# Running the 256-column half of an accumulating matmul unit first where the unit before ended on the same width

## The chip, the cores and the metric

The kernel runs on one core of one Trainium2 chip. Five engines work beside each other: TensorE (PE, matrix products; its weight loads are shown apart as PEld), VectorE (DVE), ScalarE (ACT), GpSimd (POOL) and SyncE (SP, which here only issues DMAs). The metric is the device time of one execution in microseconds, the median of several runs.

## The reference

One layer of a streaming encoder over 512 tokens of width 2048, all in fp32. Cut to what matters:

```python
hn   = rmsnorm(x, norm_g)                          # 512 x 2048
proj = einsum('bsd,dc->bsc', hn, w_in)             # 12 x 512 columns q,k,v,gate of 3 branches,
                                                   # 4 forget logits, 3 x 2048 merge-gate columns
ya = forgetting_attention(qa, ka, va, f_logit)     # branch A: softmax with forget bias
yb = chunked_relpos_attention(qb, kb, vb, rel)     # branch B: softmax over a band, relative bias
yc = stick_breaking_attention(qc, kc, vc)          # branch C
ys = stack([ya, yb, yc]) * silu(gate)
up = einsum('bsnw,nwd->bsnd', ys, w_up)            # 3 products 512 -> 2048
merged = sum(sigmoid(merge_gates) * up)
return x + einsum('bsd,de->bse', merged, w_out)    # 2048 -> 2048
```

Nearly all the work is in three dense products: the input projection (2048 by some 12,300 columns), the up-projection and the output projection.

## The kernel before

**Precision by parts.** An fp32 operand is split in two fp32r parts, a high part (`wh` of the weights, rounded by ACT, line 243) and the rest, the low part (`wl`, by DVE as the difference, line 247). A product is high x high + high x low + low x high. For one 128 x 128 block of weights that is a matmul with 512 moving columns for the high weights (256 columns of the operand's high part and 256 of its low part, which lie side by side) and one with 256 columns for the low weights (the operand's high part alone). The first kind is called wide here, the second narrow. All of them are issued in `mm`, line 261, so the profile shows them on line 262, the wide ones with `wh` and the narrow ones with `wl` among their tiles.

**Tiling.** Input and output projections work on pairs of 128-column blocks with a Strassen-like scheme over 2 x 2 blocks of 1024 by 256: seven products instead of eight. `PairTask` is one such pair of column blocks; its seven `Pair` units, one per product, are numbered 1 to 7. A unit has eight steps `j` along the contraction: eight wide matmuls into a PSUM bank, then, once the low weights are there (`yield u.ready`), eight narrow ones into the left half of the same bank. Since the halves of the operand are summed up later, the bank holds two 256-column halves that are folded together when it is read.

**Order and banks.** The usual order of a pair's units is 1, 2, 6, 5, 7, 3, 4. Unit 6 adds onto the bank that unit 1 has left open, 7 onto 6, 4 onto 7, and 3 onto 5 (the table `onto` in `mms_of`); between two such units the bank is read as it stands, by ACT or DVE (`after_of`), and the later unit waits for that reading (`yield self.ev[onto]`). The units 1, 2 and 5 open a bank and clear it with their first matmul (`start`). One of the gate pairs has the order 1, 5, 6, 2, 7, 3, 4 (`x1_first`). Two pairs, the first gate pair and the first output pair, are `late`: their seven units use the banks in turn, don't add on, and issue 24 matmuls of 256 columns each, sixteen with the high weights and eight with the low ones. `single` units do that as well: all units of the late pairs, and unit 4 of the last output pair (`plain_end`).

**Stages.** First the q, k, v and gate columns of one head, taken straight without the scheme; then for the other eleven heads a pair for q and k, a pair of gate columns, a pair for v and the branch gate, and a pair of gate columns, 28 units a head (24 pairs of gate columns in all); then the up-projection, 32 units of 512-column matmuls alone; then eight output pairs. The attention of a head is spread over the units that follow it.

**What sets the order.** The instruction lists of PE, ACT and DVE are written in the order that a planner finds (`Flow`). It has a clock for each of the three engines, costs for the instructions (`mm_us`, `act_us`, `dve_us`) and due times, and always takes the operation that can start first. `stream` (line 1519) goes through the units one after the other and lets attention work slip in between any two matmuls; at unit `i` it starts `prep` of unit `i + 2`, the split of its weights. `wh` and `wl` have three buffers each, which the planner does not count. Raw weights come in by DMA into six tiles, issued on SP's queue; the weights of product 5 and of product 7, sums of two blocks, are added up in the transfer, on POOL's queue. On the chip only the semaphores count; an engine that is early runs ahead of the plan as far as its list allows.

Of the kernel before, what the change touches and what calls it, by code (L numbers as in the profile page):

```python
# [16 lines left out]
S = 512  # L17
# [8 lines left out]
UK = 8  # L26
NQ = 4
HS = S // 2
# [7 lines left out]
PE, ACT, DVE = 0, 1, 2  # L36
# [26 lines left out]
class Flow:  # L63
# [19 lines left out]
    def spawn(self, gen, slack, ready=None):  # L83
        task = Task(gen, slack, self.now if ready is None else ready)
        self.tasks.append(task)
        self.advance(task)
# [62 lines left out]
def mm_us(n, x=1):  # L149
    return x * max(0.115, n / 2400 + 0.0133)  # L150
# [11 lines left out]
def hybrid_kernel(  # L162
# [16 lines left out]
    wp = ctx.enter_context(tc.tile_pool(name="wp", bufs=3))  # L179
    tp = ctx.enter_context(tc.tile_pool(name="tp", bufs=NT))  # L180
    sp = ctx.enter_context(tc.tile_pool(name="sp", bufs=8))
# [10 lines left out]
    flow = Flow()  # L192
    spawn, set_, give = flow.spawn, flow.set, flow.give
    t2s, atts, raws, xps = Slots(NT, KEPT), Slots(4), Slots(NR), Slots(NX)
    accs = [Slots(2), Slots(1), Slots(1)]
# [7 lines left out]
    def acc(i=0):  # L203

        return pa.tile([P, S], F32, tag=f"acc{i}", name=nm("acc"), bufs=1 if i else 2)
# [10 lines left out]
    LH, RH = slice(0, HS), slice(HS, S)  # L216

    def two(ap):

        return ap.rearrange("p (h s) -> p h s", h=2)  # L220

    class Parts:


        def __init__(self, s, ev=None):
            self.t = xp.tile([P, 2, 2, HS], F32R, tag="x", name=nm(s))
            self.hi, self.lo = self.t[:, :, 0, :], self.t[:, :, 1, :]
            self.ev = ev or [Event(), Event()]
# [32 lines left out]
    def mm(ps, w, x, start=False, stop=False, more=False):  # L261
        nc.tensor.matmul(ps, w, x, start=start, stop=stop, skip_group_check=more)  # L262
# [10 lines left out]
    first = []  # L273
# [77 lines left out]
    class Unit:  # L351


        def __init__(self, mms, after=None, shape=(UK, P), srcs=()):
            self.shape, self.mms, self.after, self.srcs = list(shape), mms, after, srcs
            self.ready_hi, self.ready, self.there, self.raw = Event(), Event(), Event(), None

        def source_there(self):
            return self.there
# [24 lines left out]
    def prep(u):  # L384
        n = u.shape[0] * P
        u.hi = wp.tile([P] + u.shape, F32R, tag="wh", name=nm("wh"), bufs=LA + 1)
        u.lo = wp.tile([P] + u.shape, F32R, tag="wl", name=nm("wl"), bufs=LA + 1)
        yield u.source_there()
        yield from split(u.hi, u.lo, u.source(), n, u.ready, hi_ev=u.ready_hi)
        u.split_done()  # L390
# [168 lines left out]
    class Pair(Unit):  # L559


        def __init__(self, task, i):
            super().__init__(task.mms_of(i), task.after_of(i))
            self.task, self.p = task, task.order[i]

        def source_there(self):
            if self is self.task.units[0]:
# [10 lines left out]
    class PairTask:  # L578
# [57 lines left out]
        def mms_of(self, i):  # L636
            p = self.order[i]
            bank = (0, 1, 2, 0, 0, 1, 2)[i] if self.late else {2: 1, 5: 2, 3: 2}.get(p, 0)
            onto = None if self.late else {6: 1, 7: 6, 4: 7, 3: 5}.get(p)
            more = onto is not None  # L640
            single = self.late or self.plain_end and p == 4
            self.bank = getattr(self, "bank", {})
            self.bank[p] = bank

            def go(u):
                if more:
                    yield self.ev[onto]
                    self.ps[p] = self.ps[onto]
                else:
                    yield accs[bank], 1  # L650
                    self.ps[p] = acc(bank)

                for j in range(UK):
                    yield lambda: self.ops[p](j) is not None
                    r, _, ev = self.ops[p](j)
                    yield ev
                    if single:
                        yield PE, mm_us(HS)
                        mm(self.ps[p][:, LH], u.hi[:, j, :], r[:, 0, :], j == 0 and not more, more=more)
                    else:  # L660
                        yield PE, mm_us(S)
                        mm(two(self.ps[p]), u.hi[:, j, :], r, j == 0 and not more, more=more)
                    if single:
                        yield PE, mm_us(HS)
                        mm(self.ps[p][:, LH], u.hi[:, j, :], r[:, 1, :], more=more)
                yield u.ready
                for j in range(UK):
                    yield PE, mm_us(HS)
                    mm(self.ps[p][:, LH], u.lo[:, j, :], self.ops[p](j)[1], stop=j == UK - 1, more=more)
            return go  # L670

        def after_of(self, i):
# [844 lines left out]
            yield from load_unit(u)  # L1517

    def stream():
        for i, u in enumerate(units):  # L1520
            cur[0] = i
            for g in side.pop(i, ()):
                spawn(g(), 5.0, flow.fin)
            for j in range(LA + 1) if i == 0 else (i + LA,):
                if j < len(units):
                    spawn(prep(units[j]), 2.5, flow.fin)
            yield u.ready_hi
            yield from u.mms(u)
            if u.after is not None:
                spawn(u.after(), 0.0, flow.fin)  # L1530
# [6 lines left out]
    for k in range(UK):  # L1537
        spawn(combos(k), 5.0)
    spawn(stream(), 1e9)
    flow.run()  # L1540
    assert not side, side


NT = 21
KEPT = 1
NX = 28
NR = 6
# [47 lines left out]
```

## Time and profile before

| | |
|---|---|
| median of three runs | 1331.93 us (1330.86 to 1333.83) |
| the profiled execution | 1331.46 us, its span 1329.7 us |
| PE busy | 1317.4 us, 99% of the span |
| PE weight loads busy | 1149.0 us, 86% |
| DVE busy | 1134.5 us, 85% |
| ACT busy | 806.3 us, 61% |
| PE in the chain of waits that ended last | 98% |
| DMA | 266.24 MB, mean 200 GB/s |
| wide matmuls on `wh` into pair banks, mean of one | 0.39 us |
| narrow matmuls on `wl`, mean of one | 0.28 us |

The busy share of PE is an overlap of pipelined instructions: a narrow matmul is shown with 0.28 us although the next one starts 0.12 us later. For the pace one reads the starts in the timeline, not the durations. In the timeline, rows with the same tiles and shape are merged: the first number is the start of the first, the second the time from there to the end of the last, and xN their count.

The profiled execution took 1331.46 us, of which 1329.7 are its span from the first to the last instruction and 1.8 lie around it; it is 0.5 us below the median.

### The profile page before, as it was taken

The numbers are of one execution on the slowest core, as the hardware profiler recorded it, in microseconds if no ns is written. First come the engines' busy times: TensorE is split into PE (matmuls) and PEld (weight loads), VectorE is DVE, ScalarE is ACT, GpSimd is POOL, SyncE is SP. The second block draws the span as 40 slices with busy tenths as digits, with TensorE's granted clock in tenths as the row PEclk, the third lists the DMA queues.
The fourth block names the chain that finished last, engine by engine and source line by source line (L and its number), as shares of the span: only waits on it lengthen the run. The fifth ranks groups of instructions, "written<-read, shape, count | busy, mean of one in ns | idle before, by whom it ended". The sixth has DMA issues, their size and how long they took to land.

```text
span 1329.7 us, 20204 instructions
## 1 busy us (share of the span) xinstructions
PE 1317.4 (99%) x7490; PEld 1149.0 (86%) x7490; DVE 1134.5 (85%) x1675; ACT 806.3 (61%) x1280; POOL 94.8 (7%) x120
## 2 busy tenths in 40 slices
PE   8999999999999999999999999999999999999998
PEld 5888888888888888888888888888888888888887
DVE  7899888788888889888988979888899877897786
ACT  8777557575566665666556665666557655454443
POOL 0000000010000100000010100001000000000100
PEclk9999999999999999999999999999999999999999
DMA  9876677767776777767777677676768856668883
GB/s 312 230 188 171 187 201 188 199 171 200 195 209 165 205 204 184 212 158 210 202 182 205 163 207 200 188 202 175 198 179 273 276 193 193 186 173 241 238 238 108
DMA packets 93251, 266.24 MB, mean 200 GB/s; under 512 B 10576, under 2 KB 17360, under 8 KB 93152
## 3 DMA queue, kind: packets, MB, share of 16 engines
q1 hardware_dynamic: 73472, 203.79, 45.6%
q0 software_dynamic: 15552, 56.63, 24.9%
q10 hardware_dynamic: 4128, 4.53, 1.0%
q8 instruction: 59, 0.97, 0.3%
q14 instruction: 40, 0.33, 0.1%
HBM read 245.21 MB, written 19.70 MB: 199 GB/s over the span
## 4 chain that ended last, share of the span: by engine, by line
PE 98%; DVE 1%; DMA 0%; issue 0%; ACT 0%; DVEq 0%
PE acc L262 84%; PE att L262 8%; PE att L998 1%; PE att L257 1%; PE att L258 1%; PE att L1111 1%; PE att L1112 1%; PE att L259 1%; PE att L1110 1%; DVE wl L247 0%; PE att L1062 0%; DMA raw<-in_w_col 0%; PE att L1213 0%; PE att L899 0%; PE att L900 0%; DVE m L247 0%
## 5 line engine op out<-in xcount | busy, mean ns | idle before, releaser
L247 DVE TENSOR_TENSOR wl<-raw,wh 128x1024 fp32r<-128x1024 f32 (+2 forms) x419 | 500.7, 1198 | 145.0 <-ACT wh L243 137.7
L243 ACT ACTIVATE wh<-raw 128x1024 fp32r<-128x1024 f32 (+2 forms) x419 | 434.7, 1038 | 149.3 <-PE acc L262 61.9
L262 PE MATMUL acc<-x,wh 128*128 128x512 f32 (+1 forms) x1568 | 399.4, 391 | 6.8 <-ACT wh L243 6.8
L262 PEld LDWEIGHTS acc<-x,wh 128*128 128x128 f32 x1568 | 277.6, 190 | 55.8 <-ACT wh L243 7.2
L262 PE MATMUL acc<-t,wh 128*128 128x512 f32 (+1 forms) x1128 | 283.8, 390 | 0.0
L262 PEld LDWEIGHTS acc<-t,wh 128*128 128x128 f32 x1128 | 198.3, 189 | 32.8
L262 PEld LDWEIGHTS acc<-x,wl 128*128 128x128 f32 x1504 | 207.0, 190 | 18.0 <-DVE wl L247 1.7
L262 PE MATMUL acc<-x,wl 128*128 128x256 f32 (+1 forms) x1504 | 217.0, 285 | 0.6 <-DVE wl L247 0.6
L262 PEld LDWEIGHTS acc<-t,wl 128*128 128x128 f32 x1104 | 151.7, 190 | 11.4
L262 PE MATMUL acc<-t,wl 128*128 128x256 f32 x1104 | 155.5, 283 | 0.0
L282 POOL DMA_DIRECT2D raw<-in_w_col x92 | 79.5, 864 | 926.7 <-DMA raw<-in_w_col 529.7
L262 PE MATMUL acc<-m,wh 128*128 128x512 f32 (+1 forms) x512 | 113.7, 366 | 1.5 <-DVE m L247 1.5
L262 PEld LDWEIGHTS acc<-m,wh 128*128 128x128 f32 x512 | 85.5, 190 | 14.4 <-DVE m L247 1.9
L805 ACT ACTIVATE c<-acc 128x256 f32<-128x256 f32 x51 | 19.5, 383 | 97.2 <-PE acc L262 94.2
L772 ACT ACTIVATE u<-acc 128x512 f32<-128x512 f32 x51 | 30.3, 594 | 79.4 <-PE acc L262 79.4
L751 ACT ACTIVATE u<-acc 128x512 f32<-128x512 f32 x52 | 31.1, 598 | 72.2 <-PE acc L262 69.3
L627 DVE TENSOR_TENSOR raw<-raw,raw 128x1024 f32<-128x1024 f32 x54 | 65.9, 1220 | 0.5
L621 DVE TENSOR_TENSOR raw<-raw,raw 128x1024 f32<-128x1024 f32 x54 | 65.9, 1220 | 0.4
L262 PE MATMUL att<-y,wh 128*128 128x512 f32 x256 | 65.8, 389 | 0.0
L262 PEld LDWEIGHTS acc<-m,wl 128*128 128x128 f32 x448 | 60.6, 191 | 3.8
L262 PE MATMUL acc<-m,wl 128*128 128x256 f32 x448 | 62.5, 282 | 0.0
L262 PEld LDWEIGHTS att<-y,wh 128*128 128x128 f32 x256 | 48.1, 188 | 10.0
(191 smaller groups left out, 1389.8 us busy)
## 6 DMA issues: line engine op xcount, KB each, us to landing
raw<-in_w_col SPq DMA_DIRECT2D x237, 512.0 KB, 4.3
raw<-in_w_col POOLq DMA_DIRECT2D x92, 512.0 KB, 6.5
raw<-in_w_out SPq DMA_DIRECT2D x40, 512.0 KB, 4.0
gl<-c SPq DMA_DIRECT2D x48, 256.0 KB, 3.6
raw<-in_w_up SPq DMA_DIRECT2D x32, 384.0 KB, 3.8
sg<-gl SPq DMA_DIRECT2D x48, 256.0 KB, 5.1
raw<-in_w_out POOLq DMA_DIRECT2D x16, 512.0 KB, 6.1
x<-in_xT SPq DMA_DIRECT2D x16, 256.0 KB, 6.4
```

Source lines behind the costliest of these rows:

```text
L243: nc.scalar.activation(hi, src, AF.Copy)
L247: nc.vector.tensor_sub(lo, src, f(hi))
L257: nc.tensor.matmul(ps, lh, rh, start=start, stop=False, skip_group_check=more)
L258: nc.tensor.matmul(ps, lh, rl, start=False, stop=False, skip_group_check=more)
L259: nc.tensor.matmul(ps, ll, rh, start=False, stop=stop, skip_group_check=more)
L262: nc.tensor.matmul(ps, w, x, start=start, stop=stop, skip_group_check=more)
L282: nc.gpsimd.dma_start(to, src, accum_op=ALU.add)
L621: nc.vector.tensor_add(w[1], w[1], w[5])
L627: nc.vector.tensor_add(w[2], w[2], w[1])
L751: nc.scalar.activation(self.u, ps, AF.Copy)
L772: nc.scalar.activation(self.s, ps, AF.Copy)
L805: nc.scalar.activation(c, ps[:, RH], AF.Copy, scale=-1.0)
```

## The change

A unit gets a flag `low_first`. Where it is set, the unit issues its eight narrow matmuls first and its eight wide ones behind them; otherwise wide first, as before. `mms_of` is rewritten around two inner functions, `high` and `low`, which get told whether they come first, for the `start` and `stop` marks. `stream` sets the flag for a unit just before it is issued: the unit adds onto an open bank, the unit before ended with narrow matmuls, and the low weights have been ready for 0.4 us by the planner's clock. `single` and `onto` move from the closure to the unit. Nothing else is touched: the same matmuls, operands, banks and loads.

```diff
             self.ready_hi, self.ready, self.there, self.raw = Event(), Event(), Event(), None
+            self.low_first = False
...
             self.task, self.p = task, task.order[i]
+            self.single = task.late or task.plain_end and self.p == 4
+            self.onto = None if task.late else {6: 1, 7: 6, 4: 7, 3: 5}.get(self.p)
...
-                for j in range(UK):
-                    yield lambda: self.ops[p](j) is not None
-                    r, _, ev = self.ops[p](j)
-                    yield ev
-                    if single:
...
-                yield u.ready
-                for j in range(UK):
-                    yield PE, mm_us(HS)
-                    mm(self.ps[p][:, LH], u.lo[:, j, :], self.ops[p](j)[1], stop=j == UK - 1, more=more)
+                def high(first):
+                    for j in range(UK):
+                        yield lambda: self.ops[p](j) is not None
+                        r, _, ev = self.ops[p](j)
+                        yield ev
+                        start, stop = first and j == 0 and not more, not first and j == UK - 1
...
+                            yield PE, mm_us(S)
+                            mm(two(self.ps[p]), u.hi[:, j, :], r, start, stop, more)
+
+                def low(first):
+                    yield u.ready
+                    for j in range(UK):
+                        yield lambda: self.ops[p](j) is not None
+                        _, x, ev = self.ops[p](j)
+                        yield ev
                         yield PE, mm_us(HS)
+                        mm(self.ps[p][:, LH], u.lo[:, j, :], x, first and j == 0 and not more,
+                           not first and j == UK - 1, more)
+
+                steps = (low, high) if u.low_first else (high, low)
+                for first, step in zip((True, False), steps):
+                    yield from step(first)
             return go
...
     def stream():
+        ends_low = False
...
             yield u.ready_hi
+            if isinstance(u, Pair) and not u.single:
+                low_there = u.ready.t is not None and u.ready.t + AHEAD <= flow.clock[PE]
+                u.low_first = ends_low and u.onto is not None and low_there
+                ends_low = not u.low_first
+            else:
+                ends_low = False
             yield from u.mms(u)
...
+AHEAD = 0.4
```

More of the change, by code (lines that the diff above doesn't have):

```diff
@@ L638, in mms_of @@
             bank = (0, 1, 2, 0, 0, 1, 2)[i] if self.late else {2: 1, 5: 2, 3: 2}.get(p, 0)
-            onto = None if self.late else {6: 1, 7: 6, 4: 7, 3: 5}.get(p)
-            more = onto is not None
-            single = self.late or self.plain_end and p == 4
             self.bank = getattr(self, "bank", {})
@@ L645, in go @@
             def go(u):
+                single, onto = u.single, u.onto
+                more = onto is not None
                 if more:
@@ L651, in go @@
                     self.ps[p] = acc(bank)
-                for j in range(UK):
-                    yield lambda: self.ops[p](j) is not None
-                    r, _, ev = self.ops[p](j)
-                    yield ev
-                    if single:
-                        yield PE, mm_us(HS)
[L659 to L663, printed above, removed]
-                        yield PE, mm_us(HS)
-                        mm(self.ps[p][:, LH], u.hi[:, j, :], r[:, 1, :], more=more)
@@ L666, in go @@
-                yield u.ready
-                for j in range(UK):
-                    yield PE, mm_us(HS)
-                    mm(self.ps[p][:, LH], u.lo[:, j, :], self.ops[p](j)[1], stop=j == UK - 1, more=more)
+                def high(first):
[4 more added lines that the diff above has]
+                        start, stop = first and j == 0 and not more, not first and j == UK - 1
+                        if single:
+                            yield PE, mm_us(HS)
+                            mm(self.ps[p][:, LH], u.hi[:, j, :], r[:, 0, :], start, stop, more)
+                            yield PE, mm_us(HS)
+                            mm(self.ps[p][:, LH], u.hi[:, j, :], r[:, 1, :], more=more)
+                        else:
+                            yield PE, mm_us(S)
+                            mm(two(self.ps[p]), u.hi[:, j, :], r, start, stop, more)
@@ L1527, in stream @@
             yield u.ready_hi
+            if isinstance(u, Pair) and not u.single:
+                low_there = u.ready.t is not None and u.ready.t + AHEAD <= flow.clock[PE]
+                u.low_first = ends_low and u.onto is not None and low_there
+                ends_low = not u.low_first
+            else:
+                ends_low = False
             yield from u.mms(u)
```

## The prediction

> **What bounds the kernel now.** I read the page first (busy shares, granted clock, chain of waits), then the busy time by stretches, then TensorE's (PE's) waits, and then the timeline of PE alone, where the price of the change stands.
>
> ```profile
> span 1329.7 us, 20204 instructions
> PE 1317.4 (99%) x7490; PEld 1149.0 (86%) x7490; DVE 1134.5 (85%) x1675; ACT 806.3 (61%) x1280; POOL 94.8 (7%) x120
> PEclk9999999999999999999999999999999999999999
> ```
>
> ```profile
> 64.00:1036.00 972.00, 971.20 (x5684) 855.36 (x5683) 845.51 (x1231) 613.34 (x974) 76.78 (x89) 1.00 0.72 195
> ...
> 1180.00:1329.70 149.70, 144.82 (x851) 128.04 (x849) 115.80 (x151) 63.67 (x76) 11.21 (x13) 1.00 0.72 205
> ```
>
> ```profile
> PE acc L262 <- ACT wh L243: 6.8, 2, 6.6
> PE acc L262 <- DVE m L247: 1.5, 2, 1.3
> PE acc L262 <- DVE wl L247: 0.6, 1, 0.6
> ```
>
> In the 972 us that hold all but one of the column pairs PE is busy for 971.20, at a granted clock of 1.00. In the whole span it waits 8.9 us for other engines, and the longest of those waits lie at the start and at the first output pair. So the time is the length of PE's instruction stream, and whatever shortens this stream reaches the end undiminished, as long as VectorE (DVE, 85% busy) keeps delivering the weights. The stalls at the start and the tail behind the last matmul are not touched by the change.
>
> A busy PE says nothing about pace, so the timeline of starts comes next. This is the plain stretch of ten units, nothing put between them:
>
> ```profile
> 623.66 2.00 PE L262 MATMUL acc<-t,wh 128*128 128x512 f32 x8
> 625.50 1.12 PE L262 MATMUL acc<-t,wl 128*128 128x256 f32 x8
> 626.45 2.00 PE L262 MATMUL acc<-x,wh 128*128 128x512 f32 x8
> ...
> 651.59 0.22 PE L257 MATMUL att<-qkh,qkh 128*128 128x128 f32 x1
> ```
>
> The first column is the start. Eight 512-column matmuls take 625.50 - 623.66 = 1.84 us, eight 256-column ones 626.45 - 625.50 = 0.95 us, and ten units take 651.59 - 623.66 = 27.93 us: **2.793 us a unit**. Now the same widths where they do not alternate. The gated up-projection issues 512 columns only, the first output pair 256 columns only. The first row below is from the chain of waits, the others from the timeline.
>
> ```profile
> 1038.99 5.44 PE att L262 x24
> ```
>
> ```profile
> 1169.54 2.08 PE L262 MATMUL acc<-m,wh 128*128 128x256 f32 x16
> 1171.46 1.12 PE L262 MATMUL acc<-m,wl 128*128 128x256 f32 x8
> ...
> 1181.06 2.08 PE L262 MATMUL acc<-m,wh 128*128 128x256 f32 x16
> ```
>
> 24 wide matmuls in 5.44 us are 226.7 ns each. From 1169.54 to 1181.06 lie four units of 24 narrow ones, 11.52 us or 120.0 ns each. At these paces a unit would take 8 x 226.7 + 8 x 120.0 = 2773.6 ns. It takes 2793, so **one turn from narrow to wide and back costs 19.4 ns**, wholly in the wide part (1.84 against 1.814 us, so some 26 ns lost there; the narrow part is some 10 ns quicker than its steady pace). Both steady stretches cross unit boundaries, weight buffers and banks too, so it isn't the boundary that costs, but the alternation.
>
> The Trainium skill, "TensorE: Matmul & The Clock Gate", section "Back-to-back issue gap", gives an isolated matmul a gap of N/2.4 + 2.5 ns, by its own width alone; an estimate from that is 8 x 215.8 + 8 x 109.2 = 2600 ns for a unit in any order, and the change would save nothing. The trace does not agree in either respect: 2793 ns, and a unit whose cost depends on its neighbours. The same section also says that in a stream of weight loads and matmuls both set the spacing, which fits better.
>
> **The change, part by part.** (1) *Turns removed.* A normal pair runs its units in the order 1, 2, 6, 5, 7, 3, 4. Units 6, 7, 4 and 3 add onto an open bank. The rule makes a unit start with its narrow run only if the unit before ended narrow, so the string of a pair goes from HL HL HL HL HL HL HL (H wide, L narrow) to HL HL LH HL LH HL LH: seven turns become four, at 6, 7 and 4 three fall away. There are 22 column pairs, 24 gate pairs and 8 output pairs; the first gate pair and the first output pair are `late` and excluded, and in the last output pair unit 4 is `single`. That is 52 x 3 - 1 = 155 turns. The gate pair in the order 1, 5, 6, 2, 7, 3, 4 also loses three.
>
> (2) *The condition.* A unit is turned round only if the planner's clock has its low weights ready 0.4 us ahead. The planner's clock is not in the trace, but what really happened is. I set the k-th low-weight split on DVE against the k-th unit on PE over all 156 units 6, 7 and 4. In 114 of them the low weights are there over 2 us before the unit begins, in 18 they are less than 0.53 us early, and none is late. The first of the 18 (a DVE row and a PE row), the last, and the shortest of all:
>
> ```profile
> 382.17 1.22 DVE L247 TENSOR_TENSOR wl<-raw,wh 128x1024 fp32r<-128x1024 f32 x1
> ...
> 383.86 1.32 PE L262 MATMUL acc<-t,wh 128*128 128x512 f32 x5
> ```
>
> ```profile
> 1031.76 1.22 DVE L247 TENSOR_TENSOR wl<-raw,wh 128x1024 fp32r<-128x1024 f32 x1
> ...
> 1033.29 2.00 PE L262 MATMUL acc<-t,wh 128*128 128x512 f32 x8
> ```
>
> ```profile
> 731.92 1.22 DVE L247 TENSOR_TENSOR wl<-raw,wh 128x1024 fp32r<-128x1024 f32 x1
> ...
> 733.38 2.00 PE L262 MATMUL acc<-t,wh 128*128 128x512 f32 x8
> ```
>
> The first split ends at 383.39 and its unit begins at 383.86, 0.47 us later. The second is 0.31 us early, the third 0.24. If the condition refuses all of the 18 and nothing else, 155 - 18 = 137 turns go; if none, 155. I take 141, nearer to the lower end since the planner's figure for a 1024-column split, 1.175 us, leaves DVE no more slack than the trace does. 141 x 19.4 ns = **2.7 us**; the ends are 2.66 and 3.0 us.
>
> (3) *Weights needed earlier.* In a turned unit the low weights are needed 1.84 us earlier than now, and the one wait of 0.6 us for them in the rows above shows how much room there was. A price of nothing rests on the leads in (2). If the lead were short by x, PE would stand for x in that unit; I take 0 for the 137, and 0 to 0.2 us each for up to 18 tight ones (0.4 us is the margin asked, 0.24 the shortest lead seen), so 0 to 3.6 us at the far end, 0.1 us in the sum.
>
> (4) *Buffers freed at other times.* High and low weights rotate through three buffers each. A turned unit gives its low buffer back 1.84 us sooner and its high buffer 0.95 us later, since the wide run ends the unit. The third unit after it then gets its ACT split (`wh`, 1.05 us) up to 0.95 us later, and behind that its DVE split, the return of the raw tile, and the load (on SP's queue, or POOL's for the summed ones) that waits for this tile. What hides it: ACT's split now begins over two units before its use where nothing queues, and where the lead is tight the split has been waiting for DVE rather than for ACT:
>
> ```profile
> 463.06 0.38 ACT L805 ACTIVATE c<-acc 128x256 f32<-128x256 f32 x1 [2.49 <-PE acc L262]
> 463.34 1.05 ACT L243 ACTIVATE wh<-raw 128x1024 fp32r<-128x1024 f32 x1
> ```
>
> ```profile
> 466.76 1.22 DVE L247 TENSOR_TENSOR wl<-raw,wh 128x1024 fp32r<-128x1024 f32 x1
> ```
>
> ```profile
> 468.45 2.00 PE L262 MATMUL acc<-t,wh 128*128 128x512 f32 x8
> ```
>
> This is a unit 6 with 0.47 us of lead. Its high split stood behind an ACT copy that waited for the end of the unit 4 three places before (462.86), so the high buffer of that unit, freed 0.95 us later, would not have moved it, and it was done 2.4 us before DVE came to it. Loads: ACT's splits wait only 5.4 us in the whole span for arriving weights, so I price a later load at 0 as well.
>
> ```profile
> DMA raw<-in_w_col: 5.4, 4
> ```
>
> (5) *Attention work put between.* Where the planner slips score or transpose matmuls into a unit, they would fall after about five narrow matmuls of a turned unit instead of after three wide ones. Both cases are in the trace with the same work (three 128-column products and a mask):
>
> ```profile
> 282.05 0.86 PE L262 MATMUL acc<-x,wh 128*128 128x512 f32 x3
> ...
> 283.07 1.38 PE L262 MATMUL acc<-x,wh 128*128 128x512 f32 x5
> 284.30 1.12 PE L262 MATMUL acc<-x,wl 128*128 128x256 f32 x8
> ```
>
> ```profile
> 113.72 0.64 PE L262 MATMUL acc<-x,wl 128*128 128x256 f32 x4
> ...
> 114.52 0.72 PE L262 MATMUL acc<-x,wl 128*128 128x256 f32 x4
> 115.08 0.86 PE L262 MATMUL acc<-t,wh 128*128 128x512 f32 x3
> ```
>
> Inside the wide run it lengthens it by 284.30 - 282.05 - 1.84 = 0.41 us, inside the narrow run by 115.08 - 113.72 - 0.95 = 0.41 us: no difference. The plan shifts as a whole, though, and how often a group splits a run can change by some; ten groups more or fewer, at the 20 to 30 ns by which a split run loses its pace, are ±0.3 us.
>
> (6) The operands, the number of matmuls, the banks, the copies out of the banks (at the end of a unit either way), the DMAs and the tail are the same: 0.
>
> **Sum.** -2.7 + 0.1 = -2.6 us against the profiled execution: 1331.46 (span 1329.7 and 1.8 around it) becomes 1328.8. That execution is 0.5 below the median of the runs, 1331.93, so for the median I say **1329.2 us**. A change of 0.2%, 2.7 us, is about what a measurement of this kernel tells from none; the three runs before lie 3 us apart. The forecast sits on that bound.
>
> **Rivals.** *The order buys nothing* (a matmul costs by its own width, the rule weighed above, or the loss at a turn belongs to the weight load that a unit begins with and comes back in another place). For it: 19 ns is small and I see it as a difference of paces between stages. Against: the up stage and the first output pair keep their steady paces through many unit boundaries. Time: 1331.9, give or take 0.5.
>
> *The condition refuses many.* The planner may see DVE later than it really is. If it passes only half, 78 x 19.4 ns = 1.5 us: 1330.4. For it: DVE is 85% busy in truth and the planner's price of a split is a little above the 1.13 us between back-to-back ones (466.76 above to the next instruction at 467.89). Against: three quarters of the leads exceed 2 us.
>
> ```profile
> 467.89 1.22 DVE L627 TENSOR_TENSOR raw<-raw,raw 128x1024 f32<-128x1024 f32 x1
> ```
>
> *Slower: a held high buffer makes unit 6 wait.* Unit 6 is three places behind unit 4 of the pair before, which is turned and frees its high buffer 0.95 us later; the planner doesn't count these buffers. If DVE's split moved by all of that, every unit 6 with under 1.07 us of lead would stall PE: 14 of the 52, by 0.95 + 0.12 us less its lead, in sum 5.2 us. With the turns saved: 1331.9 - 2.7 + 5.2 = 1334.4. It decides once the average wait of a turned unit passes 19 ns. Against it are the rows in (4).
>
> **How the numbers follow.** Forecast 0.58, the order buys nothing 0.22, many refused 0.11, a stall 0.09. Within the forecast case I leave about one in ten to a smaller count and to run-to-run scatter that hides it: faster by over 0.2%: 0.52. Within 0.2%: the rest of that case, with the two middle rivals, 0.39. Slower: 0.09. The range: at the low end 3.0 us saved and the 1.1 us by which the lowest run lies under the median, 1327.8; at the high end the case of no gain, 1332.1. The forecast's own range is 1328.3 to 1330.3.
>
> **What would show it.** In the timeline of PE, a plain pair of seven units should take 19.49 us instead of 19.55, with runs of narrow matmuls of unit 6, 7 or 4 directly behind the narrow runs of 2, 5 and 3, and a wide run behind a turned unit in 1.81 us, not 1.84. The first wide run behind sixteen narrow ones should still take 1.84. PE's waits for `wl` should stay under 1 us; over 3 us there mean the stall. The number of narrow runs that begin a unit tells the count in (2). ACT's waits before `wh` for PE should grow from the 61.9 us of before, at no cost. If the runs are joined and the wide run still takes 1.84 us, the price of a turn was misread.
>
> ```profile
> ACT wh L243 <- PE acc L262: 61.9, 57, 3.0
> ```

## The result and the profile after

The changed kernel takes 1329.93 us (median of 20 runs, 1329.11 to 1331.68), the kernel before 1332.66 in the same number of runs: a ratio of **0.998, 95% interval 0.9973 to 0.9986**, 2.7 us less. The profiled execution took 1330.04 us, its span 1328.3.

The page of after, and PE's waits:

```profile
span 1328.3 us, 20244 instructions
PE 1314.9 (99%) x7490; PEld 1149.2 (87%) x7490; DVE 1135.6 (85%) x1675; ACT 807.9 (61%) x1280; POOL 94.8 (7%) x120
```

```profile
PE acc L262 <- ACT wh L243: 7.9, 3, 6.6
PE acc L262 <- DVE m L247: 1.5, 2, 1.3
PE acc L262 <- DVE wl L247: 0.6, 1, 0.6
```

The same 7490 matmuls, and PE waits for low weights as little as before, 0.6 us: one wait at 71 us, in the first gate pair, where nothing is turned. The joined runs stand in the timeline of the output stage; seven units from the second unit of a pair to that of the next, first after, then before:

```profile
1191.03 2.00 PE L262 MATMUL acc<-m,wh 128*128 128x512 f32 x8
1192.87 2.08 PE L262 MATMUL acc<-m,wl 128*128 128x256 f32 x16
1194.78 3.82 PE L262 MATMUL acc<-m,wh 128*128 128x512 f32 x16
1198.44 2.08 PE L262 MATMUL acc<-m,wl 128*128 128x256 f32 x16
...
1210.52 2.00 PE L262 MATMUL acc<-m,wh 128*128 128x512 f32 x8
```

```profile
1191.97 2.00 PE L262 MATMUL acc<-m,wh 128*128 128x512 f32 x8
1193.81 1.12 PE L262 MATMUL acc<-m,wl 128*128 128x256 f32 x8
...
1211.52 0.86 PE L262 MATMUL acc<-m,wh 128*128 128x512 f32 x3
```

Seven units take 19.49 us after (1210.52 - 1191.03) and 19.55 before. Sixteen wide matmuls take 1198.44 - 1194.78 = 3.66 us where twice eight took 3.68. Counted over all starts, an undisturbed wide run (no attention work within or beside it) behind a narrow one loses 27.4 ns and a narrow run behind a wide one wins 7.5, in both kernels and, to 2 ns, whether the runs have eight or sixteen: 20 ns a turn, three turns a pair, 60 ns.

By stages, from the first wide matmul of the second pair (after, then before), of the up-projection and of the second output pair to the last narrow run:

```profile
81.95 0.86 PE L262 MATMUL acc<-x,wh 128*128 128x512 f32 x3
...
1035.16 1.98 PE L262 MATMUL acc<-y,wh 128*128 128x512 f32 x8
...
1188.24 2.00 PE L262 MATMUL acc<-m,wh 128*128 128x512 f32 x8
...
1323.84 1.12 PE L262 MATMUL acc<-m,wl 128*128 128x256 f32 x8
```

```profile
80.83 0.86 PE L262 MATMUL acc<-x,wh 128*128 128x512 f32 x3
...
1036.08 2.00 PE L262 MATMUL acc<-y,wh 128*128 128x512 f32 x8
...
1189.17 2.00 PE L262 MATMUL acc<-m,wh 128*128 128x512 f32 x8
...
1325.17 1.12 PE L262 MATMUL acc<-m,wl 128*128 128x256 f32 x8
```

| stretch | before | after | difference |
|---|---|---|---|
| start to the second pair | 80.83 | 81.95 | +1.12 |
| column and gate pairs | 955.25 | 953.21 | -2.04 |
| up-projection, first output pair | 153.09 | 153.08 | -0.01 |
| output pairs to the last narrow run | 136.00 | 135.60 | -0.40 |

The start, whose instructions are the same in all kernels here, varies from one execution to the next; over the twelve profiles with this stream (all but e8 and e9) the time from the first matmul to the second pair lies between 72.5 and 75.6 us. The change itself is the two rows in which units were turned: **-2.44 us**. I counted 136 turned units: 41 of product 6, 44 of 7, 43 of 4, and 8 of product 3.

### The profile page after: what moved, and what is told of

Read it like the earlier page. It is cut to its first block, busy times and chain, and to the rows that moved or that the text cites. A ratio compares the mean times of both kernels' runs of the same rounds, so it can differ in the third digit from the quotient of the medians.

```text
span 1328.3 us, 20244 instructions
## 1 busy us (share of the span) xinstructions
PE 1314.9 (99%) x7490; PEld 1149.2 (87%) x7490; DVE 1135.6 (85%) x1675; ACT 807.9 (61%) x1280; POOL 94.8 (7%) x120
## 4 chain that ended last, share of the span: by engine, by line
PE 97%; DVE 1%; DMA 1%; issue 0%; ACT 0%; DVEq 0%; ACTq 0%
PE acc L262 83%; PE att L262 8%; DMA raw<-in_w_col 1%; PE att L1011 1%; PE att L257 1%; PE att L258 1%; PE att L1124 1%; PE att L1125 1%; PE att L259 1%; PE att L1123 1%; DVE wl L247 0%; PE att L1075 0%; PE att L1226 0%; PE att L912 0%; PE att L913 0%; DVE m L247 0%
## 5 line engine op out<-in xcount | busy, mean ns | idle before, releaser
L243 ACT ACTIVATE wh<-raw 128x1024 fp32r<-128x1024 f32 (+2 forms) x419 | 434.7, 1038 | 167.1 <-PE acc L262 73.5
L262 PEld LDWEIGHTS acc<-x,wh 128*128 128x128 f32 x1568 | 284.1, 189 | 64.1 <-ACT wh L243 8.6
L262 PE MATMUL acc<-t,wh 128*128 128x512 f32 (+1 forms) x1128 | 280.9, 388 | 0.0
L262 PE MATMUL acc<-t,wl 128*128 128x256 f32 x1104 | 158.5, 284 | 0.0
L262 PEld LDWEIGHTS acc<-t,wl 128*128 128x128 f32 x1104 | 145.2, 191 | 2.1
L262 PE MATMUL acc<-m,wh 128*128 128x512 f32 (+1 forms) x512 | 109.9, 365 | 1.5 <-DVE m L247 1.5
L262 PE MATMUL acc<-m,wl 128*128 128x256 f32 x448 | 59.4, 283 | 0.0
```

What stands on the lines that cost most here:

```text
L243: nc.scalar.activation(hi, src, AF.Copy)
```

## The experiments

All are set against the kernel before. The numbers for the pairs are the time from the second pair to the up-projection, as in the table's second row (955.25 us before in all three of its profiles).

**Shorter runs (e1).** Each plain unit as four wide, four narrow, four wide, four narrow.

```diff
+                run = UK if single else RUN      # RUN = 4
+                for k in range(0, UK, run):
+                    js = range(k, k + run)
+                    yield from high(js)
+                    yield from low(js)
```

> The kernel before, with each plain unit in two halves: four wide matmuls, four narrow, four wide, four narrow. Some 363 units get one turn more. Theory (a turn from narrow to wide and back has a price of its own, which falls on the first wide matmuls behind it): the first four wide ones carry some 23 of the 27 ns that a wide run loses, and the narrow run wins back 6, so each added turn costs about 16 ns: +6 us, about 1338.5 against 1332.7, a ratio near 1.0045. Rival (the order buys nothing, a matmul costs by its own width): 1.000. A doubled turn at the full 20 ns would be +7.3 us.

Measured: 1335.89 us against 1332.61, a ratio of 1.0017 (1.0008 to 1.0027). The pairs take 957.93, +2.68, and the output stage +0.63. The timeline of its output stage:

```profile
1230.13 1.09 PE L262 MATMUL acc<-m,wh 128*128 128x512 f32 x4
1231.06 0.63 PE L262 MATMUL acc<-m,wl 128*128 128x256 f32 x4
...
1235.74 0.63 PE L262 MATMUL acc<-m,wh 128*128 128x512 f32 x2
```

Two units take 1235.74 - 1230.13 = 5.61 us, 2.805 each against 2.793. More turns cost time, so the order matters and the rival falls. The size missed: the added 9 ns a unit (3.31 us over 363) are less than the 16 I expected. Counted over all starts, a run of four wide ones loses 21.6 and its narrow run wins 6.0, so a turn costs 15.6; I had added one such turn to a full one, but two short ones (31) replace one long one (20), which gives 11.

**Alternating (e2).** The same with `RUN = 1`.

> The kernel before, with wide and narrow matmuls in turn at every one of the eight steps of a plain unit. Seven turns more in each of some 363 units. If every turn had the full price of 20 ns: +140 ns a unit, +51 us, a ratio of 1.038. If the price lies in a settling of the first wide matmuls behind a narrow run, and only the first position counts: a first wide one takes 233 ns and a first narrow one 114, together 347 a step against 349 in the kernel before, 2776 instead of 2793 ns a unit: -6 us, a ratio near 0.9955. The low weights are needed 1.84 us earlier in all units, and the shortest lead seen is 0.14 us, so waits for them should stay small (under 3 us in sum). If the order buys nothing: 1.000.

Measured: 1336.03 us, a ratio of 1.0022 (1.0012 to 1.0032); the pairs 957.48, +2.23. From its output stage:

```profile
1202.15 0.40 PE L262 MATMUL acc<-m,wh 128*128 128x512 f32 x1
1202.38 0.28 PE L262 MATMUL acc<-m,wl 128*128 128x256 f32 x1
...
1205.68 0.40 PE L262 MATMUL acc<-m,wh 128*128 128x512 f32 x1
```

Ten steps take 3.53 us, 353 ns each; a step at the two steady paces is 226.7 + 120.0 = 346.7. Both expectations miss. Neither is the price of a turn constant (+51 us), nor does it shrink to the first position's (-6 us). A turn costs 4 to 6 ns here (350.7 ns a step over all starts, 353 in this stretch), 15.6 with runs of four and 20 with eight or sixteen. In an undisturbed wide run the intervals are 233, 236, 228, 232 and 231 ns, then 227: the loss builds up over the first five wide matmuls behind a turn and then stops. PE's wait for low weights stays at 0.6 us. The gain of the change is the number of turns in the regime where each has its full price.

**Without the condition (e3, again as e6).**

```diff
-                u.low_first = ends_low and u.onto is not None and low_there
+                u.low_first = ends_low and u.onto is not None
```

> The changed kernel without the condition that the low weights be there 0.4 us ahead: every unit 6, 7 and 4 behind a narrow run is turned, 155 turns instead of 136. Theory (real leads are enough, 0.24 us at the shortest): PE's waits for low weights stay under 1 us and the 19 turns save 0.3 to 0.4 us more, a ratio near 0.9977. Rival (tight units stall once low weights are needed at once, and the condition is what pays): 0.1 to 0.4 us for each of the 19, waits for low weights of 2 to 8 us, slower than the changed kernel by 2 us or more.

> Without the condition, once more: 155 turns fewer. By 18 ns a turn 2.8 us below before (0.9979), 0.3 us below the changed kernel. Waits of PE for low weights under 1 us. If the 1.5 us that this kernel lost at the start of the output stage belong to it (and not to a clock that happened to be lowered behind the stall there), they come again: the first output pair and the pairs behind it 160.5 us instead of 159.0.

Measured: 1328.76 us, 0.9977 (0.9967 to 0.9987), and the second time 1330.51 against 1331.96, 0.9984 (0.9976 to 0.9993). 155 units are turned; the pairs take 952.73 us in both, 0.48 less than in the changed kernel. PE's wait for low weights in the first run:

```profile
PE acc L262 <- DVE wl L247: 0.2, 1, 0.2
```

(0.6 in the second; both are the one wait in the first gate pair.) No unit stalls although all of the tight ones are turned. So the leads of 0.24 us and more are enough, as step (3) of the prediction had it, and the condition protects from nothing in this kernel. What the first profile lost at the output stage is told at the end.

**Openers too (e4), and every second unit (e7).** Units 1, 2 and 5 may be turned as well: their first narrow matmul clears the bank, and the wide ones then write the right half and add onto the left. e4 keeps the condition, e7 drops it.

```diff
-                u.low_first = ends_low and u.onto is not None and low_there
+                u.low_first = ends_low and low_there        # e4
+                u.low_first = ends_low                      # e7
```

> The changed kernel with the rule extended to units 1, 2 and 5, which open a bank: a unit that follows a narrow run starts narrow, whichever it is (its first narrow matmul clears the bank). Every second unit would be turned, some 175 to 182 turns instead of 136. Theory: 40 to 46 turns more at 18 to 20 ns, 0.7 to 0.9 us below the changed kernel, a ratio near 0.9973 to the kernel before. Rival (units that start a pair are tighter, and PE waits): no gain over the changed kernel, or waits for low weights over 1 us.

> The changed kernel once more, beside the two that follow, so that the three are compared on the same chip: 136 turns fewer than before, a ratio of 0.998. If the profile shows a full clock behind the stall at the first output pair, the output stage takes 136.4 us.

> Both together: no condition, and units that open a bank are turned as well, so that every second plain unit starts narrow, some 182 turns fewer than before. Theory (18 to 20 ns a turn, leads are enough): 3.3 to 3.6 us below before, a ratio of 0.9973 to 0.9975, 0.9 us below the changed kernel, waits for low weights under 1 us. Rival (with units 1, 2 and 5 needing their low weights at once, the 0.14 us of the shortest unit 2 no longer do): waits for low weights of 1 us or more, and no gain over the changed kernel.

e4: 161 turned, not 175 to 182; 1328.7 us, 0.997 (0.9958 to 0.9982); the pairs 952.46. On another chip, beside each other: the changed kernel again (e5) 1330.84 us, 0.9991 (0.9983 to 1.0); e6, given above; e7 1329.91, 0.9979 (0.997 to 0.9987), with 181 turned and the pairs at 952.58. The changed kernel gains only 1.1 us there, where 0.998 was expected and 2.7 us had been measured; its pairs take 953.21 us as before, so the missing part does not lie in them. PE waits for low weights 0.6 us in e4, e5 and e7 alike, so the tight first and second units don't stall either. The 20 turns more that e7 has over e4 bring nothing in the pairs: 137 turns there save 2.79 us in e4, 157 save 2.67 in e7. Which runs attention work splits differs from plan to plan (45 groups of it split a wide run and 40 a narrow one in e4, 53 and 35 in e7), and a turn at a split run need not cost 20 ns; that this is the reason is not shown. e7 lies 0.9 us below the changed kernel of the same runs, but the intervals overlap; that it is better is likely, not shown.

**What in a narrow run slows the wide run (e8, e9).** The low-weight matmuls take 128 or 384 columns instead of 256 (in e8 half of that product is left out, in e9 a wrong one is added).

```diff
+                    x = self.ops[p](j)[0].rearrange("p a b -> p (a b)")[:, :n]     # n = 128, 384
+                    mm(self.ps[p][:, :n], u.lo[:, j, :], x, stop=j == UK - 1, more=more)
```

> The kernel before with the low-weight matmuls cut to 128 columns (half of that product is left out). This asks what in a narrow run slows the wide run behind it. If it is the change of width, or the narrow run being as quick as the weight loads allow: the first five wide matmuls take 233, 236, 228, 232, 231 ns again or longer, 27 ns or more lost a unit. If it is the narrow run's own 256-column form: something else. A narrow matmul takes 110 to 120 ns if the load of its weights binds it, 67 ns if its width does.

> The kernel before with the low-weight matmuls widened to 384 columns (128 columns of a wrong product are added). If the loss comes from the change of width as such, the wide run behind still loses some 27 ns. If it comes from narrow matmuls being nearly as short as the load of the next weights, 384 columns (some 173 ns each) leave room and the wide run goes at 226.7 ns from the first on. The stream gets 2900 x 53 ns = 155 us longer either way.

One execution of each: 1317.82 and 1500.51 us. The timelines, e8 first:

```profile
1217.90 2.07 PE L262 MATMUL acc<-m,wh 128*128 128x512 f32 x8
1219.80 1.00 PE L262 MATMUL acc<-m,wl 128*128 128x128 f32 x8
1220.64 2.07 PE L262 MATMUL acc<-m,wh 128*128 128x512 f32 x8
```

```profile
1400.93 2.01 PE L262 MATMUL acc<-m,wh 128*128 128x512 f32 x8
1402.78 1.58 PE L262 MATMUL acc<-m,wl 128*128 128x384 f32 x8
1404.20 2.01 PE L262 MATMUL acc<-m,wh 128*128 128x512 f32 x8
```

Behind 384 columns the eight wide matmuls take 1402.78 - 1400.93 = 1.85 us, 37 ns over the steady 1.813, more than behind 256. A narrow matmul takes 177 ns here ((1404.20 - 1402.78) / 8), and a narrow run with that much time for each weight load still slows the wide one. So it is not the cause that narrow matmuls are nearly as short as the load; the change of width is what is left. The change from high to low weights isn't the cause either: the up-projection changes between them too, at one width, and its 24 matmuls in 5.44 us lose nothing.

Behind 128 columns the eight take 1.90 us; there the second wide one follows the first only after 284 ns (233 behind 256 columns), and the narrow ones come every 105 ns on average, although their width alone would make it 67 by an estimate (120.0 less 128 columns at (226.7 - 120.0) / 256 ns each): with 128 columns something other than the width binds, and the weight load, the only other work of each step on PE, is the likely one.

Counted over all undisturbed runs, the wide series is 233 236 228 232 231 227 ns behind 256 columns and 229 233 236 224 231 236 228 233 behind 384. Behind 128 columns it is 284 233 236 224 231 236 228 232, from the second on nearly the same as behind 384. So behind both of these the pace has not settled at 227 within eight, as it has after five behind 256 columns. Why a change of width starts this stays open.

**The kernel before twice more and the changed one once more (e10 to e12).**

> The kernel before, looked at once more. The profiles with turned units show a granted clock of 0.83 for some microseconds behind the stall at the first output pair in five of six cases, those without turned units never in three. If the lowered clock comes with the turned units, the full 1.00 stands here again in the ten microseconds behind the stall, and the output stage takes 136.8 us; if it is chance, 0.83 and some 1.5 us more.

> The same again: 1.00 behind the stall if the lowered clock comes with the turned units, either of the two if it is chance.

> The changed kernel, a third look. Its two profiles showed 1.00 and 0.83 behind the stall. The first stretch up to the second pair, in which its instructions are those of the kernel before, takes 72 to 76 us whatever the kernel; from there to the up-projection 953.2 us against 955.25 before, in every profile within 0.1 us.

1332.8, 1333.81 and 1329.82 us. The pairs take 955.25, 955.25 and 953.21 us, as in the other profiles of the same kernels: the gain is the same to 0.1 us in each execution. e11, which has no turned unit, shows the lowered clock behind the stall, as e8, which has none either, had done; e12, which has 136, doesn't. So it doesn't come with the turned units.

## Why the prediction was right

**The time.** 1329.2 was said, 1329.93 measured, with the kernel before at 1332.66 in these runs and not 1331.93. The sum of the prediction is -2.6 us, which from the median gives 1329.3; 1329.2 is what comes without the 0.1 us of part (3). The medians lie 2.73 us apart, and the profiles show 2.44 in the stages concerned. That the medians agree with 2.7 to a few hundredths is luck: the count and the mean price of a turn were both taken too high, the start alone varies by 3 us between executions, and in e5 the same kernel gained 1.1. The mechanism was right, and its size in the profiles, 2.44 us, is a tenth below 2.7.

**(1) Turns removed: right, with the count and the price a little off.** The price in undisturbed pairs is 20.0 ns, not 19.4. In the column and gate pairs it is only 2.04 us / 116 turns = 17.6 ns. In total the wide runs of this stage lose 9.8 us instead of 14.3, a gain of 4.5 where 116 turns at 27.4 ns explain 3.2, and the narrow ones lose 0.4 instead of winning 2.0, a loss of 2.4 where 116 turns at 7.5 ns explain 0.9. Attention matmuls that used to split wide runs now split narrow ones: of these groups, 68 stood within a wide run and 13 within a narrow one, and now 55 and 26. That this accounts for the difference is read from the sums, not tried by itself. If it does, part (5), which found no difference between the two places, looked at one pair of cases and was too coarse by these 2.4 ns a turn, 0.3 us in all, the edge of its own bound of ±0.3.

**(2) The condition: 136 turned, 141 said,** and one fewer than the lower end of 137. The condition refused 19 units (11 of product 6, 8 of product 7), where the leads had let me expect 18 at most. The leads did show most of them: 14 of the 19 are among the 18 tight ones, four of the other five had leads of 0.87 us and one of 1.56. What I overlooked is product 3: where 7 is refused and ends narrow, 3 is turned instead, and then 4 follows a wide run and isn't. Eight times a 3 took the place of a 4.

**(3) Low weights needed earlier: right**, no wait added; the experiment without the condition shows that there was room even for the tight ones, so the 0.1 us in the sum should have been 0. The wait of 0.6 us that this part took as a sign of the room lies in the first gate pair, where no unit can be turned, and says nothing about it; the leads do.

**(4) Buffers freed at other times: right.** ACT's splits wait longer for PE, 73.5 us instead of 61.9, and PE does not wait for them in turn: its waits for high weights, 7.9 us, all lie before the second pair, where nothing is turned. The slower rival, unit 6 stalled by the held high buffer, didn't occur in any kernel, not even with all units 6 turned.

```profile
ACT wh L243 <- PE acc L262: 73.5, 68, 2.4
```

**The rivals.** "The order buys nothing" fell with the 60 ns a pair and with e1. "The condition refuses many" fell with 136 turns of 155. The rule of the Trainium skill that was set against the trace ("TensorE: Matmul & The Clock Gate", "Back-to-back issue gap", a gap from a matmul's own width) is not borne out: the same wide matmul follows its predecessor by 226.7 ns in a run of its kind and by up to 236 behind a run of 256 columns.

## What to carry to other kernels

When one engine is busy for 99% of the span, read its pace from the starts, compare each shape's pace in a run of its own with its pace in a mixture, and price the turns: here 20 ns each, saved by letting neighbouring units share a run. Such a gain is exact in the trace and nearly lost in the timing, so add up the stages concerned instead of comparing spans. Before adding a safety condition, look at the leads in the trace, and try the kernel without it.

## What was not expected of the hardware

**The clock behind a stall.** In the first output pair PE waits for operands (two waits, 1.5 us by the profile) and issues slowly around them. In some executions the granted clock is lowered just behind it. The same kernel, before, in two executions (e10, then e11), from the last narrow run of the first output pair:

```profile
1189.55 1.12 PE L262 MATMUL acc<-m,wl 128*128 128x256 f32 x8
1190.51 2.00 PE L262 MATMUL acc<-m,wh 128*128 128x512 f32 x8
```

```profile
1189.12 1.87 PE L262 MATMUL acc<-m,wl 128*128 128x256 f32 x8
1190.79 2.83 PE L262 MATMUL acc<-m,wh 128*128 128x512 f32 x8
```

and the ten microseconds around it by stretches (clock in the third place from the right), in the same order:

```profile
1185.00:1195.00 10.00, 8.53 (x52) 7.35 (x51) 9.82 (x17) 3.02 (x4) 0.86 (x1) 1.00 0.80 170
```

```profile
1185.00:1195.00 10.00, 8.53 (x43) 7.33 (x43) 9.38 (x17) 2.53 (x3) 0.86 (x1) 0.83 0.76 166
```

Some wide matmuls of e11 follow each other by 427 ns instead of 227, and the first output pair and the ones behind it take 1.5 us more. The lowered clock of e11 is one stretch at one half:

```profile
1189.15:1192.57 3.42, 3.42 (x14) 3.03 (x14) 3.42 (x5) 1.01 (x1) 0.86 (x1) 0.50 0.47 144
```

The lowered clock is seen in e3 to e8 and e11, and not in the first profiles of before and after, nor in e1, e2, e9, e10, e12. So the loss that e3 showed at the output stage came again in e6, as the expectation for the kernel's own fault had it, but in e5 too, which is the changed kernel, and in e11, the kernel before: it belongs to none of them. The Trainium skill, "TensorE: Matmul & The Clock Gate", section "Part 1: The HAM clock gate (the "warmup" mystery)", says that a free-running window decides on half the clock, so that the same kernel meets it at another phase from run to run; the doubled interval and the difference between e10 and e11 agree.

The traces also show when it comes. In the clock records of all 14 profiles each stretch of one clock, except the last, which is cut off, lasts a whole number of times 3.413 us (in e11 345 such windows at the full clock, one at half, 41 at the full clock). Laid over the stall, the emptiest window of this grid holds 9 to 12 matmul starts in the seven profiles with the lowered clock, and the clock falls at its end; in the other seven it holds 13 to 17. An undisturbed window of the first output pair holds 28. The stall itself is the same in all (1.58 us between two starts, 0.44 between two others 1 us earlier): what differs is how it lies in the grid.

The times of the runs fit this. Of the 26 runs of the kernel before that stood beside e1 to e4, 13 had a mean granted clock of 1.000 and a median of 1331.50 us, and 13 had 0.999 and 1333.48. Within a kernel the profiled executions differ in the start (72.5 to 75.6 us) and in this clock, while the pairs between agree to 0.01 us; together that is more than the whole change is worth.

**The price of a turn is not a constant.** 4 to 6 ns with runs of one, 15.6 with four, 20 with eight and with sixteen.
